# Smaller first input blocks, norm rows and convolution loads moved, and an up weight fetched sooner in a streaming encoder layer

## The chip, the cores and the metric

The kernel runs on one core of a Trainium2 chip. The metric is the time of one execution on the device, in microseconds; several runs are made of a kernel and their median is given. A core has a matrix engine (TensorE, PE in the profile), three engines for elementwise work (VectorE, DVE; ScalarE, ACT; GpSimd, POOL), and SyncE (SP), which here only issues transfers between the device's memory and the on-chip memory. Each engine works through its own list of instructions in order; semaphores make one wait for another. A transfer can be issued from SP's, ACT's or POOL's list.

## The reference

One layer of an encoder is applied to 1024 rows of a prompt and 32 rows of a sample (1056 in all, D = 1024), which share the weights. Cut to what matters:

```python
h = rms_norm(x, g_mix)
q, k, v, ch, cb, cc, ga, gb = split(h @ w_in)
a  = window_attn(q, k, v, sink) @ w_attn_out          # 16 query heads, 4 key heads
bo = (cb * causal_conv3(cc * ch)) @ w_conv_out
x  = x + (sigmoid(ga) * a + sigmoid(gb) * bo) @ w_mix_out
cq = rms_norm(x, g_cross) @ w_cq                      # 4 heads, 256 memory tokens
x  = x + softmax_attn(cq, mem_k, mem_v) @ w_co
x  = x + square(relu(rms_norm(x, g_mlp) @ w_up)) @ w_down
y  = rms_norm(x, g_final)
```

The new keys, values, convolution rows and memory keys and values are returned too. Everything is float32.

## The kernel before

The 1056 columns (tokens lie along the free axis, features on the 128 partitions) are cut into three chunks of 384, 384 and 288 columns, `CH[0]` to `CH[2]`. A float32 product is made of three products of the faster type fp32r: each operand is split into a rounded part hi (a cast on ACT) and the rest lo (a subtraction on DVE), and PE adds hi·hi, hi·lo and lo·hi. So each weight block of 128x1024 goes through a load (tile `wr`), a cast (`wh`, L129) and a subtraction (`wl`, L130), and each activation tile likewise (`X`, `Y`, `N`, `M`, `Z`). `gemm` (L191) makes 8 x 3 matmuls for one output block of 128 features and one chunk.

The stages in order: the input norm and K, V, Q (`norm_x`); windowed attention; the attention's output; the gate products (one pair of gate blocks for each f from 0 to 7; from f = 1 on by a scheme with seven products in place of eight, in which sums of weight blocks, `g_sum`, made earlier on POOL and kept in memory, meet sums of activation tiles, kinds `t2`, `n1`, `n3`, `n4`, `b11` and so on); the convolution's output and the mixing product of each chunk (`do_conv_out`, `do_mix`), woven with the memory attention of the chunk before (`do_cq`, `do_co`); then the up and down products of the MLP, in the same seven-product scheme on halves and quarters of the columns.

`item(fn, *keys)` appends a piece of work to a plan, and the list `worder` of weights that the plan needs is worked off ahead of it: `fetch_w` loads the next weight, `issue_w` splits one. Inside the stages a scheduler orders the instructions of each engine; `pin` keeps an instruction at the place where it is written, and `tc.manual_schedule` does that for all of one engine's. `tile(..., tag, bufs)` takes the next of `bufs` buffers, and waits until that buffer's last reader is done; `acc_tile` gives one of three PSUM accumulators, tag `pt` two further PSUM buffers, `tmp` a scratch buffer (`ct`).

The places that the change touches:

- `norm_x`: loads of x and of the parameters `prm` (gains and other columns), the first weight, the tables of functions of ACT, then the splits and the first products.
- `pump(n)` (L797): splits what the last call loaded, and starts n loads more from the list `wanted`; at the gates these are the tiles of `n4` (from `xs_n`) and then of the convolution (from `bc_d`), that the convolution's output reads. Gate pair f = 1 calls it three times, with 4, 4 and 0.
- The norm of a chunk: `chunk_col` sums the squares on PE into `pq` and works out one number for each column; `chunk_row` spreads it over the partitions (ACT L242, DVE L243, PE L244 and L245 into `pr`, ACT L255 into R). `do_cq` (L1111) multiplies its gemm by R afterwards.
- `do_conv_out` (L1047): a gemm, then the gate's multiplication by L1055 on DVE, the addition L1056, and the split into M. It is L1055 that empties the accumulator.
- `normed(c, f)` (L1285): the normed tile for the MLP by L1287 on DVE, its transfer to memory, and for chunk 0 its split by L1298 (ACT) and L1299 (DVE).
- The order of chunk 2's stage is written out by hand: `then(i, ...)` hangs work behind filler i (fillers 0 to 7 are chunk 2's `do_conv_out`).
- `open_second` and `up_start`: the second set of PSUM tiles and the first up weights; `up_issue(0, 4)` splits one of them. L1362 is ACT's reading of an accumulator of the products before.

Of the kernel before, what the change touches and what calls it, by code (L numbers as in the profile page):

```python
# [40 lines left out]
def hybrid_step(ctx: ExitStack, tc: tile.TileContext, io):  # L41
# [102 lines left out]
    fetched = []  # L144
    third = {}

    def fetch_w():
        if third:
            third["n"] += 1
        if third and third["n"] % 3 == 0:  # L150
            raw = third["pool"].tile([P, 4, 256], F32, tag="ws", name=nm("wr3")).rearrange("p q c -> p (q c)")
        else:
            raw = wp.tile([P, 1024], F32, tag="wr", bufs=2, name=nm("wr"))
        src = weight(worder[wpos[0] + len(fetched)])
        load = sp.dma_start(raw.rearrange("p (i c) -> p i c", i=4) if len(src.shape) == 3 else raw, src)
        if third and third["n"] == 3 and third["pool"] is W["pool"]:
            pin(load)
        fetched.append(raw)
# [130 lines left out]
    start_end = []  # L289

    def norm_x():
        pool_e.memset(ones, 1.0)
        act.copy(ones_r, ones.to_broadcast([P, P]))
        warm = misc.tile([P, 1], F32, name="warm")
        act.activation(warm, ones, AF.Sqrt)
        make_identity(nc, ident)
        raws = []

        def load_x():
            for c, (o, n) in enumerate(CH):  # L300
                raw = raw_tile()[:, : NF * n].rearrange("p (f t) -> p f t", f=NF)
                for h in range(4):
                    sp.dma_start(raw[:, 2 * h : 2 * h + 2], io[f"x{c}"][:, 2 * h : 2 * h + 2])
                    if c == h == 0:
                        sp.dma_start(prm, io["params"])
                if c == 0:
                    fetch_w()
                    fetch_w()
                raws.append(raw)

        def parts(c, fs, pinned=lambda x: x):
            for f in fs:
                xg[c][f] = (slot(xpool, f"X{c}", CH[c][1]), slot(xpool, f"X{c}", CH[c][1]))
                scaled_split(*xg[c][f], raws[c][:, f], G_MIX + f, pinned)

        def squares(c):
            n = CH[c][1]
            acc = st.tile([P, n], F32, tag="sum", bufs=2, name=nm("sum"))
            for f in range(NF):
# [6 lines left out]
        first_raw = wp.tile([P, 1024], F32, tag="wr", bufs=2, name=nm("wr"))  # L326
        with tc.manual_schedule(engines={mybir.EngineType.Activation}):
            act.dma_start(first_raw, weight(worder[0]))
# [24 lines left out]
        for c, (o, n) in enumerate(CH):  # L353
            a = acc_tile([P, n])
            gemm(a, wk, xg[c])
            act.copy(kt[:, o : o + n], a)
            if c < 2:
                parts(c + 1, range(NF), pin)
            vs3[c, 0] = v_block(wv, c, 0)
            if c:  # L360
                scaled(c - 1)
            chunk_col(c)
            vs3[c, 1] = v_block(wv, c, 1)
            vs3[c, 2] = v_block(wv, c, 2)
            if c < 2:
                squares(c + 1)
            if c == 1:
                mem_load_x()
        for key in start_keys:
            next_w(key)  # L370

        def end():
            scaled(2)
            sp.dma_start(io["o_k"][0], kt[:, 896:])
            v = tmp(256)
            sp.dma_start(v, io["cache_v"])
# [537 lines left out]
    def gate_pair(f):  # L914
# [50 lines left out]
        u2 = Y["top"].tile([P, 384], F32, tag="u2", name=nm("u2"))  # L965
        dve.tensor_sub(u2, B, s1)
        sum_step()
        pump(4 if f == 1 else 1)
        w3 = take(("g_sum", f - 1, 1))
        product(C, w3, 1, op("n1"), True)  # L970
        v = Y["top"].tile([P, 384], F32, tag="v", name=nm("v"))
# [75 lines left out]
    def do_conv_out(c, f):  # L1047
        def fn(w):
            n = CH[c][1]
            t1 = tmp(n)  # L1050
            sp.dma_start(t1, m1_d[c][:, f])
            a = acc_tile([P, n])
            gemm(a, w, bcp[c])
            t = tmp(n)
            dve.tensor_mul(t, a, sg[c][f])  # L1055
            (dve if f == NF - 1 else pool_e).tensor_tensor(t, t, t1, op=ALU.add)  # L1056
            mg[c][f] = (mslot(n), mslot(n))
            split(*mg[c][f], t)

        return fn  # L1060
# [50 lines left out]
    def do_cq(c, j):  # L1111
        def fn(w):
            n = CH[c][1]
            a = acc_tile([P, n])
            gemm(a, w, xc[c])
            t = tmp(n)
            dve.scalar_tensor_tensor(t, a, 0.125, R[c], op0=ALU.mult, op1=ALU.mult)
            for e in range(2):
                own, other = slice(64 * e, 64 * e + 64), slice(64 - 64 * e, 128 - 64 * e)
                q = yslot(c)  # L1120
                act.copy(q[own], t[own])
                dve.tensor_sub(q[other], t[own], q[own].bitcast(F32))
                qc[2 * j + e, c] = q

        return fn
# [133 lines left out]
    def open_second():  # L1259
        nonlocal ps  # L1260
        closed(Y["cm", 0])
        closed(ps_cm)
        S["b"] = ctx.enter_context(tc.tile_pool(name="b22", bufs=8, reuse_waits="tile", side="right"))
        L["cm2"], L["pool2"] = opened("late2", bufs=1, reuse_waits="tile", side="right")
        ps = ctx.enter_context(tc.tile_pool(name="ps2", bufs=1, space=PSUM, reuse_waits="tile"))

    def zslot(dt=F32R):
        return S["z"].tile([P, HT], dt, tag="Z", name=nm("Z"))
# [16 lines left out]
    def normed(c, f):  # L1285
        t = tmp(CH[c][1])
        pin(dve.scalar_tensor_tensor(t, x1[c][f], col(G_MLP + f), R[c], op0=ALU.mult, op1=ALU.mult))  # L1287
        o, n = CH[c]
        if c < 2 or f > 3:
            sp.dma_start(xn_d[:, f, o : o + n], t)  # L1290
        if c == 1:
            pool_e.dma_start(xa[1][f][1].bitcast(F32)[:, CH[0][1] - QT :], t[:, : HT - CH[1][0]])
        if c == 2:
            top[f] = t
        if c == 0:
            hi, lo = (yslot(0)[:, :QT] for _ in range(2))
            xa[0][f] = (hi, lo)
            act.copy(hi, t[:, :QT])  # L1298
            pin(dve.tensor_sub(lo, t[:, :QT], hi.bitcast(F32)))  # L1299

    def split_here(hi, lo):

# [318 lines left out]
    def cross_steps(c):  # L1621

        steps = [("call", [])]
        steps.append(("call", [lambda: chunk_stats(c)]))
# [60 lines left out]
    call = lambda fn, *args: lambda: item(lambda: fn(*args))  # L1685
    assert len(left) == 1
    then(0, *[call(x) for x in left[0][1]])
    then(1, call(chunk_stats, 1))
    then(2, *[lambda j=j: item(do_cq(1, j), ("w_cq", j)) for j in range(2)])
    for f in range(NF):  # L1690
        then(f // 2, call(normed, 0, f))
    for i, (_, calls) in zip((3, 5, 7, 9, 11, 12), cross_units(1)):
        then(i, *[call(x) for x in calls])
    then(14, lambda: item(do_co(1, 0), ("w_co", 0)))
# [6 lines left out]
        then(19 + f // 4, call(normed, 1, f))  # L1701
        then(22, call(second_split, f))
    then(19, call(chunk_col, 2))
    then(20, call(chunk_row, 2))
    then(21, lambda: item(do_cq(2, 0), ("w_cq", 0)))
    then(22, lambda: item(do_cq(2, 1), ("w_cq", 1)))
    for i, (_, calls) in zip((23, 25, 26, 28, 29, 31, 32), cross_units(2)):
        then(i, *[call(x) for x in calls])
    then(33, call(open_sums))
# [9 lines left out]
        then(43 + k, call(sums_then, k))  # L1719
    then(41, call(up_ready, 0))  # L1720
    then(43, call(up_second, 0))
    assert len(fillers) == 48
    for i, filler in enumerate(fillers):
        item(*filler)
# [4 lines left out]
    def up_start():  # L1729
        open_second()  # L1730
        up_load(0)
        up_issue(0, 4)
        second_b22()
        up_issue(0, 3)
        up_ready(1)
        up_second(1)
        up_t2(0)
# [258 lines left out]
```

## Time and profile before

| | |
|---|---|
| median of 3 runs | 1757.81 us (1757.32 to 1761.07) |
| the profiled execution | 1754.54 us |
| its span in the profile | 1752.8 us |
| granted TensorE clock, mean | 0.997 |
| PE busy | 1724.4 us, 98% |
| DVE busy | 1190.7 us, 68% |
| ACT busy | 853.7 us, 49% |
| POOL busy | 583.9 us, 33% |

A row of the waits gives the engine, what it was about to do, what released it, and then the total in us, the number of waits and the longest. A row of the time line gives start, duration (both in us), engine, line, operation, output<-inputs, sizes and a count where equal rows are taken together; in brackets stands the idle time of that engine before the instruction and what ended it. PEld is the load of a weight into PE, ACTq and SPq are issues of transfers. Matmuls overlap, so the time that one takes of PE is the distance of two starts, not its duration. A row of the windows gives the stretch and its length, the busy time of PE, PEld, DVE, ACT and POOL with their instructions, then PEclk (the granted clock, 1.00 is full), the DMA engines' share and GB/s.

### The profile page before, as it was taken

Reading aid. Unit: us, or ns where it says so; the run is one execution under the profiler, and the core shown is the slowest. Engines: PE = TensorE matmul, PEld = TensorE weight load, DVE = VectorE, ACT = ScalarE, POOL = GpSimd, SP = SyncE. Lnnn points to the kernel's source line nnn. Section 1 sums busy time; section 2 is a strip of 40 time slices with the busy share of each in tenths; the row PEclk is TensorE's granted clock in tenths of the full one; section 3 lists DMA queues with packets and bytes.
Section 4 is the critical chain, followed back from the end, with each engine's and each line's share of the span. In section 5 each row is a group of like instructions: output and inputs, shape, how many; then the busy total and the mean of one; then the engine's idle time right before and its main releaser. Section 6 shows DMA issues by size and latency. Waiting matters only on the chain.

```text
span 1752.8 us, 32573 instructions
## 1 busy us (share of the span) xinstructions
PE 1724.4 (98%) x12250; PEld 1710.3 (98%) x12250; DVE 1190.7 (68%) x2275; ACT 853.7 (49%) x1661; POOL 583.9 (33%) x667
## 2 busy tenths in 40 slices
PE   8999999999999999999999999999999999999998
PEld 8999999999999999999999999999999999999998
DVE  6776776867666656545677878787666686545675
ACT  8653533535335324334556665765444463332443
POOL 0025366443543444441225132105555410000121
PEclk9999999999999999999999999999999999999999
DMA  5243344333436888857866667775666695555554
GB/s 185 93 124 126 126 133 139 127 131 132 159 135 197 291 301 294 285 195 232 279 211 199 222 219 233 236 261 179 220 223 219 220 328 186 189 191 173 188 170 159
DMA packets 179565, 346.60 MB, mean 198 GB/s; under 512 B 18624, under 2 KB 100832, under 8 KB 179280
## 3 DMA queue, kind: packets, MB, share of 16 engines
q1 hardware_dynamic: 163360, 289.73, 50.1%
q0 software_dynamic: 15568, 53.68, 8.7%
q8 instruction: 96, 1.57, 0.4%
q10 hardware_dynamic: 480, 1.11, 0.2%
q14 instruction: 61, 0.50, 0.1%
HBM read 250.73 MB, written 93.14 MB: 196 GB/s over the span
## 4 chain that ended last, share of the span: by engine, by line
PE 53%; DMA 3%; DVE 2%; ACT 1%; POOL 1%; issue 1%; SPq 0%; DVEq 0%; POOLq 0%; ACTq 0%
PE acc L1781 6%; PE acc L1782 6%; PE acc L1783 6%; PE acc L870 6%; PE acc L871 6%; PE acc L872 6%; PE acc L196 2%; PE acc L198 2%; PE acc L197 2%; PE pc L871 2%; PE pc L872 2%; PE pc L870 2%; DMA ct<-in_x 1%; DMA ct<-m_d 1%; POOL ct L1056 1%
## 5 line engine op out<-in xcount | busy, mean ns | idle before, releaser
L129 ACT CAST wh<-wr 128x1024 fp32r<-128x1024 f32 (+1 forms) x231 | 241.6, 1046 | 411.8 <-PE acc L1782 132.2
L130 DVE TENSOR_TENSOR wl<-wr,wh 128x1024 fp32r<-128x1024 f32 (+1 forms) x231 | 295.6, 1280 | 129.5 <-ACT wh L129 127.7
L196 PE MATMUL acc<-X,wh 128*128 128x384 f32 (+1 forms) x864 | 282.7, 327 | 7.0 <-ACT wh L129 7.0
L197 PE MATMUL acc<-X,wh 128*128 128x384 f32 (+1 forms) x864 | 279.9, 324 | 0.3 <-DVE X L276 0.3
L198 PE MATMUL acc<-X,wl 128*128 128x384 f32 (+1 forms) x864 | 278.8, 323 | 0.0
L272 POOL TENSOR_TENSOR xacc<-xacc,ct 128x384 f32<-128x384 f32 (+1 forms) x56 | 76.9, 1376 | 374.9 <-ACT ct L270 373.3
L196 PEld LDWEIGHTS acc<-X,wh 128*128 128x128 f32 x864 | 163.3, 189 | 7.9 <-ACT wh L129 7.0
L197 PEld LDWEIGHTS acc<-X,wh 128*128 128x128 f32 x864 | 163.6, 189 | 1.4 <-DVE X L276 0.7
L198 PEld LDWEIGHTS acc<-X,wl 128*128 128x128 f32 x864 | 163.4, 189 | 0.1
L196 PE MATMUL acc<-Y,wh 128*128 128x384 f32 (+1 forms) x432 | 139.2, 324 | 3.4 <-DVE ct L1055 3.4
L197 PE MATMUL acc<-Y,wh 128*128 128x384 f32 (+1 forms) x432 | 139.2, 323 | 0.4 <-DVE Y L781 0.3
L198 PE MATMUL acc<-Y,wl 128*128 128x384 f32 (+1 forms) x432 | 139.2, 323 | 0.0
L1782 PE MATMUL acc<-n,wh 128*128 128x264 f32 x352 | 100.2, 285 | 0.0
L129 ACT CAST PTh<-pt 128x512 fp32r<-128x512 f32 (+3 forms) x94 | 45.9, 516 | 111.4 <-PE pt L588 110.6
L1781 PE MATMUL acc<-n,wh 128*128 128x264 f32 x352 | 100.2, 285 | 0.0
L1783 PE MATMUL acc<-n,wl 128*128 128x264 f32 x352 | 99.9, 284 | 0.0
L725 POOL TENSOR_TENSOR xacc<-xacc 128x256 f32<-128x256 f32 x100 | 87.9, 879 | 5.6 <-DMA xacc<-in_w_in 0.3
L725 POOL TENSOR_TENSOR ws<-ws 128x256 f32<-128x256 f32 x100 | 87.1, 871 | 5.6
L196 PEld LDWEIGHTS acc<-Y,wh 128*128 128x128 f32 x432 | 81.0, 188 | 4.5 <-DVE ct L1055 4.2
L197 PEld LDWEIGHTS acc<-Y,wh 128*128 128x128 f32 x432 | 81.1, 188 | 1.0 <-DVE Y L781 1.0
L198 PEld LDWEIGHTS acc<-Y,wl 128*128 128x128 f32 x432 | 81.1, 188 | 0.3 <-DMA wl<-wl_d 0.3
L574 ACT ACTIVATE S<-S,nmx 128x257 f32<-128x257 f32 (+1 forms) x132 | 64.2, 488 | 19.8 <-DVE nmx L569 18.5
(426 smaller groups left out, 5511.0 us busy)
## 6 DMA issues: line engine op xcount, KB each, us to landing
wr<-in_w_up SPq DMA_DIRECT2D x53, 512.0 KB, 4.7
wr<-in_w_in SPq DMA_DIRECT2D x52, 512.0 KB, 3.8
wr<-wsum_d SPq DMA_DIRECT2D x40, 512.0 KB, 3.5
wr<-in_w_conv_out SPq DMA_DIRECT2D x24, 512.0 KB, 4.1
wr<-in_w_mix SPq DMA_DIRECT2D x24, 512.0 KB, 4.9
wr<-in_w_down SPq DMA_DIRECT2D x24, 512.0 KB, 3.5
n_d<-Z SPq DMA_DIRECT2D x32, 264.0 KB, 4.3
xacc<-in_w_down POOLq DMA_DIRECT2D x16, 512.0 KB, 4.4
```

Of the source, the lines that this page charges most:

```text
L129: act.copy(hi, src)
L130: dve.tensor_sub(lo, src, hi.bitcast(F32))
L196: pe.matmul(out, wh[:, a], hi, start=(k == 0), stop=False)
L197: pe.matmul(out, wh[:, a], lo, start=False, stop=False)
L198: pe.matmul(out, wl[:, a], hi, start=False, stop=(k == len(acts) - 1))
L725: pin(pool_e.tensor_tensor(t[:, to], t[:, x], t[:, y], op=ALU.add))
L870: pe.matmul(acc, wh[:, a], hi, start=(start and k == 0), stop=False, skip_group_check=True)
L871: pe.matmul(acc, wh[:, a], lo, start=False, stop=False, skip_group_check=True)
L872: pe.matmul(acc, wl[:, a], hi, start=False, stop=(k == 3), skip_group_check=True)
L1781: pe.matmul(a, wh[:, s], hi, start=(t == 0 and k == 0), stop=False, skip_group_check=True)
L1782: pe.matmul(a, wh[:, s], lo, start=False, stop=False, skip_group_check=True)
L1783: pe.matmul(a, wl[:, s], hi, start=False, stop=(t == 1 and k == 7), skip_group_check=True)
```

## The change

Five edits, at separate places:

1. At the start, x's first block comes in transfers of one, one, two, two and two of its eight tiles; `prm` and the first weight (in two pieces) are issued from ACT's list ahead of the loading of its tables; four matmuls of plain float32 on a constant tile (`spin`) stand first on PE; the third weight goes to a `ws` tile.
2. In the gate pair f = 1 the second call of `pump` goes, so that the `bc_d` tiles start with f = 2.
3. `chunk_row` of a chunk is called inside `do_cq`, behind its first gemm, and no longer ahead of it.
4. For chunk 2, L1055 is pinned; the eight `normed` of chunk 0 hang behind fillers 1 to 8, one each, where two hung behind each of fillers 0 to 3; their lo part moves from DVE to POOL.
5. `up_issue(0, 4)` moves from `up_start` to filler 44, and two PSUM tiles that nothing uses are taken at the end of `open_second`.

```diff
+    def fetch_w(raw=None):          # with raw given, the weight is loaded there
...
     def norm_x():
+        spin = tmp(384)
+        dve.memset(spin, 1.0)
+        for _ in range(4):
+            pe.matmul(acc_tile([P, 384]), spin[:, :P], spin, start=True, stop=True)
         pool_e.memset(ones, 1.0)
-        act.copy(ones_r, ones.to_broadcast([P, P]))
+        first_raw = wp.tile([P, 1024], F32, tag="wr", bufs=2, name=nm("wr"))
         warm = misc.tile([P, 1], F32, name="warm")
-        act.activation(warm, ones, AF.Sqrt)
+        with tc.manual_schedule(engines={mybir.EngineType.Activation}):
+            act.dma_start(prm, io["params"])
+            for at in (slice(0, 256), slice(256, 1024)):
+                act.dma_start(first_raw[:, at], weight(worder[0])[:, at])
+            act.copy(ones_r, ones.to_broadcast([P, P]))
+            act.activation(warm, ones, AF.Sqrt)
...
-                for h in range(4):
-                    sp.dma_start(raw[:, 2 * h : 2 * h + 2], io[f"x{c}"][:, 2 * h : 2 * h + 2])
-                    if c == h == 0:
-                        sp.dma_start(prm, io["params"])
+                for a in (0, 1, 2, 4, 6) if c == 0 else (0, 2, 4, 6):
+                    b = a + 1 if c == 0 and a < 2 else a + 2
+                    sp.dma_start(raw[:, a:b], io[f"x{c}"][:, a:b])
                 if c == 0:
                     fetch_w()
-                    fetch_w()
+                    fetch_w(W["pool"].tile([P, 4, 256], F32, tag="ws", ...)...)
...
-        with tc.manual_schedule(engines={mybir.EngineType.Activation}):
-            act.dma_start(first_raw, weight(worder[0]))
...
         sum_step()
-        pump(4 if f == 1 else 1)
+        if f > 1:
+            pump(1)
         w3 = take(("g_sum", f - 1, 1))
...
-            dve.tensor_mul(t, a, sg[c][f])
+            (pin if c == 2 else lambda x: x)(dve.tensor_mul(t, a, sg[c][f]))
...
             gemm(a, w, xc[c])
+            if j == 0:
+                chunk_row(c)
...
         ps = ctx.enter_context(tc.tile_pool(name="ps2", ...))
+        ps.tile([P, 512], F32, tag="pt", bufs=2, name=nm("pc"))
+        wide_tile()
...
-            pin(dve.tensor_sub(lo, t[:, :QT], hi.bitcast(F32)))
+            pool_e.tensor_tensor(lo, t[:, :QT], hi.bitcast(F32), op=ALU.subtract)
...
-    then(1, call(chunk_stats, 1))
+    then(1, call(chunk_col, 1))
...
-        then(f // 2, call(normed, 0, f))
+        then(1 + f, call(normed, 0, f))
...
-    then(20, call(chunk_row, 2))
-    then(21, lambda: item(do_cq(2, 0), ("w_cq", 0)))
-    then(22, lambda: item(do_cq(2, 1), ("w_cq", 1)))
+    then(20, lambda: item(do_cq(2, 0), ("w_cq", 0)))
+    then(21, lambda: item(do_cq(2, 1), ("w_cq", 1)))
...
+    then(44, call(up_issue, 0, 4))
...
     def up_start():
         open_second()
         up_load(0)
-        up_issue(0, 4)
```

How instructions stand on three lists shows what moved. First SP's in the gate pair f = 1, before:

```order
238 L805 DMA ct_8065<-bc_d_89 128x384
239 L155 DMA wr_8160<-gsum_d 128x1024
240 L926 DMA m_d_92<-ct_7953 128x384
241 L805 DMA ct_8067<-bc_d_89 128x384
242 L805 DMA Gb_1350_7993<-xs_n_112 128x384
243 L926 DMA m_d_94<-ct_8022 128x288
244 L805 DMA Gb_1351_7995<-xs_n_112 128x384
245 L805 DMA ct_8069<-bc_d_89 128x384
246 L805 DMA ct_8071<-bc_d_89 128x384
```

and now:

```order
238 L935 DMA m_d_92<-ct_7965 128x384
239 L814 DMA Gb_1355_8005<-xs_n_112 128x384
240 L935 DMA m_d_94<-ct_8034 128x288
241 L814 DMA Gb_1356_8007<-xs_n_112 128x384
242 L943 DMA ct_8178<-a_d_107 128x384
243 L159 DMA wr_8201<-in_w_in 128x1024
```

The four loads of `bc_d` around the two loads of `xs_n` (L805 before, L814 now) are gone from here. Second PE's, the first `do_cq` gemm of chunk 0 (`pr` is the spread norm row), before:

```order
5400 L196 MATMUL acc_1823_10314<-Y0_1769_10099,wh_1794_10200 128x384
5401 L244 MATMUL pr_1808_10254<-ct_1809_10255,ones_r_75 128x384
5402 L197 MATMUL acc_1823_10314<-Y0_1770_10100,wh_1794_10200 128x384
5403 L198 MATMUL acc_1823_10314<-Y0_1769_10099,wl_1795_10201 128x384
5404 L245 MATMUL pr_1808_10254<-ct_1810_10256,ones_r_75 128x384
```

and now:

```order
5415 L200 MATMUL acc_1835_10365<-Y0_1726_9915,wh_1813_10267 128x384
5416 L248 MATMUL pr_1826_10339<-ct_1827_10340,ones_r_75 128x384
5417 L201 MATMUL acc_1835_10365<-Y0_1727_9916,wh_1813_10267 128x384
5418 L202 MATMUL acc_1835_10365<-Y0_1726_9915,wl_1814_10268 128x384
5419 L200 MATMUL acc_1835_10365<-Y0_1739_9966,wh_1813_10267 128x384
```

The product that makes `pr` stood in the first gemm and stands now in the next one (another accumulator), 15 rows later. Third DVE's, around one of chunk 2's multiplications (L1055 before, L1065 now), before:

```order
1166 L1299 TENSOR_TENSOR Y_2037_11240<-ct_11236,Y_2036_11239 128x264
1167 L1287 SCALAR_TENSOR_TENSOR ct_11243<-Ga_1708_9852,prm,R_11223 128x384
1168 L1055 TENSOR_TENSOR ct_11283<-acc_11258,Ga_1390_8187 128x288
1169 L234 SCALAR_TENSOR_TENSOR rc_11290<-st_t_11298,st_y_11297 128x3
1170 L130 TENSOR_TENSOR wl_11414<-wr_11411,wh_11413 128x1024
1171 L1299 TENSOR_TENSOR Y_2040_11247<-ct_11243,Y_2039_11246 128x264
```

and now:

```order
1169 L238 SCALAR_TENSOR_TENSOR rc_11288<-st_t_11296,st_y_11295 128x3
1170 L1301 SCALAR_TENSOR_TENSOR ct_11303<-Ga_1701_9815,prm,R_11235 128x384
1171 L1065 TENSOR_TENSOR ct_11343<-acc_11318,Ga_1415_8351 128x288
1172 L247 SCALAR_TENSOR_TENSOR ct_11384<-ident,rc_11288,ct_11383 128x128 x3
1173 L130 TENSOR_TENSOR wl_11405<-wr_11402,wh_11404 128x1024
1174 L130 TENSOR_TENSOR M_11347<-ct_11343,M_11346 128x288
```

The split of `normed` (L1299) has left DVE's list, and one product of `normed` (L1287 before, L1301 now) stands ahead of the multiplication.

More of the change, by code (lines that the diff above doesn't have):

```diff
@@ L145, in hybrid_step @@
     third = {}
-    def fetch_w():
-        if third:
+    def fetch_w(raw=None):
+        if raw is not None:
+            pass
+        elif third:
             third["n"] += 1
-        if third and third["n"] % 3 == 0:
+        if raw is not None:
+            pass
+        elif third and third["n"] % 3 == 0:
             raw = third["pool"].tile([P, 4, 256], F32, tag="ws", name=nm("wr3")).rearrange("p q c -> p (q c)")
@@ L301, in load_x @@
                 raw = raw_tile()[:, : NF * n].rearrange("p (f t) -> p f t", f=NF)
-                for h in range(4):
-                    sp.dma_start(raw[:, 2 * h : 2 * h + 2], io[f"x{c}"][:, 2 * h : 2 * h + 2])
-                    if c == h == 0:
-                        sp.dma_start(prm, io["params"])
+                for a in (0, 1, 2, 4, 6) if c == 0 else (0, 2, 4, 6):
+                    b = a + 1 if c == 0 and a < 2 else a + 2
+                    sp.dma_start(raw[:, a:b], io[f"x{c}"][:, a:b])
                 if c == 0:
                     fetch_w()
-                    fetch_w()
+                    fetch_w(W["pool"].tile([P, 4, 256], F32, tag="ws", name=nm("ws")).rearrange("p q c -> p (q c)"))
                 raws.append(raw)
@@ L324, in squares @@
             accs[c] = [acc]
-        first_raw = wp.tile([P, 1024], F32, tag="wr", bufs=2, name=nm("wr"))
-        with tc.manual_schedule(engines={mybir.EngineType.Activation}):
-            act.dma_start(first_raw, weight(worder[0]))
         fetched.append(first_raw)
@@ L1623, in cross_steps @@
         steps = [("call", [])]
-        steps.append(("call", [lambda: chunk_stats(c)]))
+        steps.append(("call", [lambda: chunk_col(c)]))
         steps.append(("items", [(do_cq(c, j), ("w_cq", j)) for j in range(2)]))
```

## The prediction

> **What bounds the kernel now.** I read the page's busy times first, then the waits of PE, then the time line at each wait, and the windows last.
>
> ```profile
> span 1752.8 us, 32573 instructions
> ...
> PE 1724.4 (98%) x12250; PEld 1710.3 (98%) x12250; DVE 1190.7 (68%) x2275; ACT 853.7 (49%) x1661; POOL 583.9 (33%) x667
> ```
>
> PE is busy for 1724.4 of 1752.8 us. The change leaves the reference's matmuls as they are and adds four, so it can only act on the 28 us in which PE is not busy, and on stretches at a lower clock. The waits of PE name where those 28 us lie:
>
> ```profile
> PE acc L196 <- ACT wh L129: 7.0, 1, 7.0
> PE acc L196 <- DVE ct L1055: 3.4, 3, 1.9
> PE acc L870 <- ACT lt L1362: 2.2, 1, 2.2
> PE pr L244 <- ACT ct L242: 1.7, 1, 1.7
> PE acc L870 <- DVE Ga L988: 1.5, 1, 1.5
> PE acc L870 <- ACT wh L129: 1.2, 1, 1.2
> ```
>
> These six rows hold 17 us in eight places, and every edit of the diff stands at one of them. A wait is seldom the whole loss: the first matmul behind it also runs longer. The profiled execution took 1754.54 us, 1.7 more than its span, and 3.3 less than the median of the runs shown (1757.81). I make the sum as a difference and take it off the median. From 0.2% on (3.5 us) a difference can be told from none.
>
> **Part 1, the start.**
>
> ```profile
> 0.73 0.41 ACTq L328 DMA_DIRECT2D wr<-in_w_in  x1
> ...
> 4.06 0.20 ACT L295 ACTIVATE warm<-ones 128x1 f32<-128x1 f32 x1
> ```
> ```profile
> 6.08 0.61 ACT L275 ACTIVATE X<-raw,prm 128x384 fp32r<-128x384 f32 x1 [1.82 <-DMA prm<-in_params]
> 6.61 1.12 ACT L129 CAST wh<-wr 128x256 fp32r<-128x256 f32 x2
> ```
> ```profile
> 6.73 0.62 DVE L276 SCALAR_TENSOR_TENSOR X<-raw,prm,X 128x384 fp32r<-128x384 f32 x1 [0.54 <-ACT X L275]
> 7.27 1.45 DVE L130 TENSOR_TENSOR wl<-wr,wh 128x256 fp32r<-128x256 f32 x2
> 8.64 3.79 DVE L276 SCALAR_TENSOR_TENSOR X<-raw,prm,X 128x384 fp32r<-128x384 f32 x7
> ```
> ```profile
> 7.05 0.69 PE L196 MATMUL acc<-X,wh 128*128 128x384 f32 x1 [7.05 <-ACT wh L129]
> ...
> 10.11 0.52 PE L196 MATMUL acc<-X,wh 128*128 128x384 f32 x1
> 10.43 0.52 PE L197 MATMUL acc<-X,wh 128*128 128x384 f32 x1
> ...
> 15.10 0.33 PE L198 MATMUL acc<-X,wl 128*128 128x384 f32 x1
> 15.27 0.28 PE L206 MATMUL acc<-wh,X 128*128 128x256 f32 x1
> ```
> ```profile
> 1050.56 0.81 PE L227 MATMUL pq<-ones,ct 128*128 128x1 f32 x6
> ```
>
> ACT waited 1.82 us for `prm`, which stood behind 384 KB of `raw` on SP's queue. Then X (0.53 us to the start of wh) and wh had to be made before PE could start at 7.05. Now `prm` goes first, and before the first product lie 192 KB of x and 128 KB of weight in place of 384 and 512. So the transfers should land near 4 us, and ACT itself becomes the limit: its work on the function tables ended at 4.26 (4.06 + 0.20), and two more DMA issues ahead of that, at 0.41 us each, make it 5.1. From there the same 0.97 us (6.08 to 7.05) leads to a first product at about 6.05: 1.0 us gained.
>
> The larger part is the clock. In the first gemm the matmuls start 0.32 us apart (10.11, 10.43), at its end 0.17 (15.10, 15.27): the 24 products took from 7.05 to 15.27, most of it at half pace. The four added matmuls fill PE from about 1.2 us on. They are plain fp32, and the trace has none of 384 columns: from 0.32 us each (the fp32r row) to 1.28 (four such passes), four take 1.3 to 5.1 us. I take the upper end: plain fp32 products leave two records each (the last row is three `pq` products), and I allow each record the columns twice. If PE is then at full speed when X arrives, the gemm is bound by DVE's lo parts instead: the first X lo can start at 5.75 (6.73 less the gain), and 0.62, 1.45 for the two pieces of wl and 3.79 for the other seven X make 11.6; PE's three products of the last X are over at 12.1, against 15.27. Next comes w_v, late by some 0.4 because its wl stands on DVE behind them. So 3.2 less 0.4 gives 2.8 us. After that PE runs gapless (29.00 busy of 29.00, the first row), so the gain is carried whole. Bounds: 1.0 if the fillers warm nothing; a loss of 0.5 if they end behind the first X.
>
> ```profile
> 15.00:44.00 29.00, 29.00 (x230) 29.00 (x229) 21.94 (x55) 24.48 (x64) 1.02 (x1) 1.00 0.34 128
> 1052.20:1055.60 3.40, 3.40 (x16) 3.40 (x15) 0.84 (x5) 1.13 (x2) 0.33 (x1) 0.50 0.42 145
> 1140.90:1144.30 3.40, 3.40 (x18) 3.40 (x17) 2.86 (x10) 1.91 (x3) 0.00 (x0) 0.51 1.02 411
> ```
>
> [...]
>
> **Part 2, the first gate pair (f = 1).**
>
> ```profile
> 677.47 0.51 ACT L800 CAST N<-Gb 128x384 fp32r<-128x384 f32 x1 [5.53 <-DMA Gb<-xs_n]
> 677.89 1.04 ACT L129 CAST wh<-wr 128x1024 fp32r<-128x1024 f32 x1
> ```
> ```profile
> 683.96 2.56 DVE L801 TENSOR_TENSOR Y<-ct,Y 128x384 fp32r<-128x384 f32 x2
> 686.43 0.54 DVE L988 TENSOR_TENSOR Ga<-acc,s 128x384 f32<-128x384 f32 x1
> ```
>
> ACT stood 5.53 us at a cast of N whose load SP had issued behind the loads of `bc_d`; the cast of wh queued behind it and PE stood 1.2 us (the last of the six rows). Seven us later DVE split two of those same `bc_d` tiles in 2.56 us, with L988 behind them, and PE stood 1.5 (the row above it). Without `bc_d` in this pair both causes go: 1.2 + 1.5, and with the longer first matmuls behind them about 0.6 more, 3.3. The eight loads and splits move to later pairs, two for each, in which none of the six rows above has a wait. Next late is N itself if its load still takes its 6 us, so I take 2.8, between 1.2 (the second wait stays) and 3.3.
>
> **Part 3, the norm row behind the first query product.**
>
> ```profile
> 889.83 0.45 PE L244 MATMUL pr<-ct,ones_r 128*128 128x384 f32 x1 [1.72 <-ACT ct L242]
> ```
>
> PE stood 1.72 us at `pr`, with gemm products that needed nothing of it behind. `pr` now comes 15 rows later in the same stream; at 0.17 us each (15.10 to 15.27 above) that is 2.6 us, which covers the wait. What reads R, the multiplication of `do_cq`, comes behind the gemm anyway. I take 1.7; bounds 0 (the row is late for R, and PSUM comes free late) and 2.0.
>
> **Part 4, the convolution's output of chunk 2** (L1055 pinned, one `normed` for each item, the lo part of it on POOL).
>
> ```profile
> 1000.50 0.82 DVE L1055 TENSOR_TENSOR ct<-acc,Gb 128x288 f32<-128x288 f32 x2
> ...
> 1001.01 0.40 PE L196 MATMUL acc<-Y,wh 128*128 128x288 f32 x1 [1.86 <-DVE ct L1055]
> 1001.09 0.81 POOL L1056 TENSOR_TENSOR ct<-ct,ct 128x288 f32<-128x288 f32 x1 [6.89 <-DVE ct L1055]
> ```
>
> L1055 frees the accumulator of a gemm, and PE waited for it three times, 3.4 us (1.86 the longest), with restarts about 3.9. Ahead of it on DVE stood the split and the product of `normed`. The split goes to POOL, eight of them; the trace has none there. The nearest row is L1056's own, 0.81 us for 288 columns, and so eight of 264 cost at most 6.5 us of POOL; DVE wins the time of its eight. Who waits for POOL: L1056 queues behind a split, and behind that the split of M and the mixing gemm, several items later. With one `normed` ahead of L1055 in place of two, I expect one of the three waits to be left in part: 2.4 gained, bounds 3.9 and -2 (rival 2).
>
> **Part 5, the up weight.**
>
> ```profile
> 1176.11 0.39 ACT L1362 ACTIVATE lt<-acc 128x264 f32<-128x264 f32 x1
> ```
>
> The first up product needed the PSUM bank that L1362 was the last to read, and L1362 stood behind two casts of a weight on ACT. The two placeholders turn the banks, so that it takes the bank which the read before that leaves, and its own weight is cast earlier. The 2.2 us go; next are the casts of the second weight, which are no earlier than before. I take 2.0, bounds 0 and 2.4.
>
> **The clock later on** I leave out of the sum. At two places PE falls to half clock for 3.4 us, each worth 1.7 us (the rows from 1052.2 and from 1140.9 above, PEclk 0.50 and 0.51). PE was not waiting there or just before; small products of one column came ahead of both. Nothing in the change takes these away, but everything shifts by some us, so one may come or go: 1.7 either way.
>
> **The sum:** 2.8 + 2.8 + 1.7 + 2.4 + 2.0 = 11.7 us. 1757.8 - 11.7 = 1746.1, rounded to 1746.
>
> **The rivals.**
>
> 1. *The middle gives back* (0.2). Between 960 and 1200 us the norms, `normed` and the memory attention of three chunks are mixed anew on all engines, and a wait may merely move. Then parts 4 and 5 bring nothing and 2.8 + 2.8 + 1.7 = 7.3 is left: 1750.5. For it: DVE is busy at 68% over all and the gaps there are single L1055s behind other work. Against it: the bank of part 5 doesn't depend on DVE.
>
> 2. *POOL becomes the late one, slower* (0.15). Eight splits of `normed` stand on POOL, in order, each behind its ACT cast. If each holds L1056 by its own 0.8 us plus the wait for that cast, the mixing gemms of chunk 2 meet late M tiles: eight waits of 1.86 us, the longest of now, are 14.9. With the 7.3 of parts 1 to 3 and nothing from parts 4 and 5 that is 7.6 slower, 1765.4. It decides from 0.9 us for each split on (eight of 0.9 use up the 7.3). Against it: POOL waited 6.89 us before its L1056, so it has room there now.
>
> 3. *The fillers don't do what they are for* (0.1): PE is still slow when X comes. Part 1 is then 1.0, the sum 9.9: 1747.9. With a loss of 0.5 there, 1749.4.
>
> **How the numbers follow.** My forecast, 0.55, has its own range of 1741 (all upper bounds, 3.2 + 3.3 + 2.0 + 3.9 + 2.4 = 14.8, and one half-clock stretch less) to 1752 (part 2 at 1.2, part 4 at none, one stretch more: 2.8 + 1.2 + 1.7 + 2.0 - 1.7 = 6.0). Nine tenths of it lie in there, 0.50, and rivals 1 and 3 almost whole, 0.27; to come to 0.8 the range goes on to 1757, a third of the way to rival 2: 1741 to 1757. Faster by over 0.2% is below 1754.3: all of the forecast, nine tenths of rivals 1 and 3, less 0.04 for parts of the forecast that fail together: 0.78. Slower is rival 2 at a little less than its whole, 0.14. The rest, 0.08, is no change.
>
> **What would show it.** In the profile of the changed kernel: first real product at 6.0 to 6.3 and the first gemm's matmuls 0.17 apart; no wait of L870 on L988 or wh near 676 to 685; no wait of `pr` near 885; at most one wait on L1055 over 1 us; no wait of 2 us at the first up product. A first gemm still 0.32 apart, or POOL rows of the new split as releasers of PE's waits for M, would make it wrong.

## The result, and the profile after

The changed kernel takes 1761.67 us in the median of 22 runs (1755.51 to 1766.14), the kernel before 1757.07 in 22 runs beside them. The ratio is 1.0023 with a 95% interval of 1.0014 to 1.0033: it is 4.1 us slower (2.5 to 5.8), where I had forecast 11.7 us faster. The two profiled executions lie 8.7 us apart, so a stage's loss in them is larger than in the mean. Ratios of the runs below are turned into us with 1756 us.

The page of the changed kernel first, and then PE's waits:

```profile
span 1761.5 us, 32594 instructions
...
PE 1734.7 (98%) x12258; PEld 1714.5 (97%) x12258; DVE 1193.1 (68%) x2268; ACT 852.0 (48%) x1661; POOL 602.4 (34%) x675
```
```profile
PE acc L202 <- DMA wl<-wl_d: 2.9, 1, 2.9
PE acc L200 <- ACT X L279: 2.0, 1, 2.0
PE acc L200 <- ACT M L129: 1.8, 1, 1.8
PE acc L879 <- DVE Ga L1080: 1.4, 1, 1.4
PE acc L299 <- DVE ct L297: 1.3, 1, 1.3
PE acc L879 <- ACT wh L129: 1.0, 1, 1.0
```

Of the six waits that the prediction began with, those for the first wh (7.0), for `pr` (1.7), for L988 (1.5) and for L1362 (2.2) are gone, the three on L1055 are one of 0.4, and a wait for a wh of 1.0 stands 8 us later than the one of 1.2. In their place stand waits for the second X, for M, for `Ga`, and for a weight's lo part. How much later the matmul at the same place of PE's list begins after than before (the four fillers left out of the count):

| place (before, us) | later by, us | what lies ahead of it |
|---|---|---|
| 18 to 120 | +1.0 to +1.2 | the start |
| 588 | +0.9 | no edit of the change |
| 690 to 837 | -0.6 | gate pair f = 1 |
| 891 | +2.7 | a wait of 2.9 for `wl`, and half clock behind it |
| 989 | +0.7 | the waits on L1055 that went |
| 1030 | +7.5 | the convolution and the mixing product of chunk 2 |
| 1190 | +7.2 | the wait for L1362 that went, and two of 0.4 and 0.8 that came |
| 1227 to the end | +9.2 to +9.0 | three waits between 1203 and 1207 (their time after) |

**The start.** PE's time line, then one row of ACT's, then the windows of 8.0 to 11.5 us:

```profile
1.32 4.82 PE L299 MATMUL acc<-ct 128*128 128x384 f32 x8 [1.32 <-DVE ct L297]
6.09 0.44 PE L200 MATMUL acc<-X,wh 128*128 128x384 f32 x1
6.46 0.44 PE L201 MATMUL acc<-X,wh 128*128 128x384 f32 x1
6.79 0.44 PE L202 MATMUL acc<-X,wl 128*128 128x384 f32 x1
9.23 0.69 PE L200 MATMUL acc<-X,wh 128*128 128x384 f32 x1 [2.00 <-ACT X L279]
...
16.24 0.28 PE L210 MATMUL acc<-wh,X 128*128 128x256 f32 x1
```
```profile
7.83 0.83 ACT L129 CAST wh<-wr 128x768 fp32r<-128x768 f32 x1 [1.78 <-DMA wr<-in_w_in]
```
```profile
8.00:8.70 0.70, 0.00 (x0) 0.00 (x0) 0.01 (x1) 0.70 (x2) 0.00 (x0) 1.00 1.06 432
8.70:9.20 0.50, 0.00 (x0) 0.00 (x0) 0.50 (x1) 0.50 (x2) 0.00 (x0) 0.53 1.00 412
9.00:11.50 2.50, 1.96 (x5) 1.56 (x6) 2.50 (x5) 2.50 (x6) 0.00 (x0) 0.50 1.02 415
```

The first product starts at 6.09 (forecast 6.05), and the fillers end in time. But ACT's order is fixed here, and next in it stands the cast of the other 768 columns of the first weight. That piece landed only at 7.7 us, ACT stood 1.78 us for it, and the second X stood behind it. PE idled 2.0 us, its clock fell to half at 8.7, and the gemm went on at 0.32 us a matmul until 15.5.

**Chunk 2's convolution.** The window of 1005 to 1037 us, where most is lost:

```profile
1005.00:1037.00 32.00, 26.58 (x180) 23.44 (x179) 26.75 (x50) 19.77 (x46) 10.47 (x11) 1.00 0.54 172
```

PE is busy for 26.58 of 32 us here; before, it was 32.00 in the same stretch. The last product of `normed` for chunk 0 stood on DVE at 1000 before; the time line of DVE now has it 24 us later:

```profile
999.98 0.61 DVE L1287 SCALAR_TENSOR_TENSOR ct<-Gb,prm,R 128x384 f32<-128x384 f32 x1
```
```profile
1024.24 0.61 DVE L1301 SCALAR_TENSOR_TENSOR ct<-Gb,prm,R 128x384 f32<-128x384 f32 x1
```

### The profile page after: what moved, and what is told of

It reads as the page before. It is cut to its first block, busy times and chain, and to the rows that moved or that the text cites. A ratio compares the mean times of both kernels' runs of the same rounds, so it can differ in the third digit from the quotient of the medians.

```text
span 1761.5 us, 32594 instructions
## 1 busy us (share of the span) xinstructions
PE 1734.7 (98%) x12258; PEld 1714.5 (97%) x12258; DVE 1193.1 (68%) x2268; ACT 852.0 (48%) x1661; POOL 602.4 (34%) x675
## 4 chain that ended last, share of the span: by engine, by line
PE 52%; DMA 4%; DVE 2%; ACT 1%; issue 1%; POOL 1%; SPq 0%; DVEq 0%; POOLq 0%; ACTq 0%
PE acc L1794 6%; PE acc L1795 6%; PE acc L1796 6%; PE acc L879 6%; PE acc L881 6%; PE acc L880 6%; PE acc L200 2%; PE acc L202 2%; PE acc L201 2%; PE pc L879 2%; PE pc L881 2%; PE pc L880 2%; DMA ct<-in_x 2%; DMA ct<-m_d 1%; DVE wl L130 1%
## 5 line engine op out<-in xcount | busy, mean ns | idle before, releaser
L734 POOL TENSOR_TENSOR ws<-ws 128x256 f32<-128x256 f32 x100 | 94.8, 948 | 5.7
```

The costliest lines, as they stand in the source:

```text
L734: pin(pool_e.tensor_tensor(t[:, to], t[:, x], t[:, y], op=ALU.add))
```

## The experiments

All runs are timed beside the kernel before. An interval of some 2 us to either side is left on each, so that only differences beyond that are told from none.

**Each part alone, on the kernel before.** The edits are those of the diff in the section on the change, one part at a time.

```diff
# e1_start: part 1, all edits of norm_x and fetch_w, of them
+            for at in (slice(0, 256), slice(256, 1024)):
+                act.dma_start(first_raw[:, at], weight(worder[0])[:, at])
# e2_gate: part 2
-        pump(4 if f == 1 else 1)
+        if f > 1:
+            pump(1)
# e3_row: part 3, with chunk_col for chunk_stats, of it
+            if j == 0:
+                chunk_row(c)
# e4_conv: part 4
+            (pin if c == 2 else lambda x: x)(dve.tensor_mul(t, a, sg[c][f]))
+            pool_e.tensor_tensor(lo, t[:, :QT], hi.bitcast(F32), op=ALU.subtract)
+        then(1 + f, call(normed, 0, f))
# e5_up: part 5, of it
+    then(44, call(up_issue, 0, 4))
```

> Only part 1 (the start) on top of the kernel before. Theory A (each part does alone what the two traces show at its place): the first gemm is over about 1.0 us later than before, since ACT casts 768 columns of the weight's second piece, which lands at 7.7 us, ahead of all further X, PE idles 2.0 us after three products and its clock falls back: +1 us in all. Rival B (what was lost arose from the five parts together): the first gemm is over 2.8 us earlier, as forecast: -2.8 us.

> Only part 2 (no second pump at f = 1). Theory A: the waits near 679 and 687 shrink by 1.5 to 2 us in all, and the gain is given back at about 872, where PE comes to a part of a weight (wl from memory) that lands at its own time: between -0.5 and +2 us over the whole. Rival B: -2.8 us, still there at 1000 us.

> Only part 3 (the norm row behind the first query product). Theory A: the wait of 1.7 us for pr at 890 goes and nothing comes in its place before 1000; between 1000 and 1100 chunk 2's cq stands one filler earlier, and what that does there is open: -2 to +1 us. Rival B: -1.7 us, no new wait over 1 us.

> Only part 4 (L1055 pinned for chunk 2, one normed for each filler, its lo part on POOL). Theory A: the three waits on L1055 shrink by 3 to 4 us, but M of chunk 2 comes late at the first mixing product and several waits of 0.5 to 3 us follow to 1037: +3 to +5 us in all. Rival B: -2.4 us.

> Only part 5 (two unused PSUM tiles taken, the first up weight's split at filler 44). Theory A (as the trace of the changed kernel shows at its place): the wait of 2.2 us for L1362 at 1176 goes, and four waits of 0.5 to 1 us come between 1184 and 1207: +0.5 to +2 us. Rival B (the wait at 1176 is not in every execution, since two runs with that place unchanged lack it): the gain is smaller than the 2.0 forecast, and the time is within 1 us of before.

| run | median, us | ratio (95%) | us |
|---|---|---|---|
| e1_start | 1757.7 | 1.0003 (0.9991 to 1.0014) | +0.5 (-1.6 to +2.5) |
| e2_gate | 1752.42 | 0.998 (0.9967 to 0.9993) | -3.5 (-5.8 to -1.2) |
| e3_row | 1755.03 | 0.9989 (0.9975 to 1.0003) | -1.9 (-4.4 to +0.5) |
| e4_conv | 1762.25 | 1.003 (1.0015 to 1.0045) | +5.3 (+2.6 to +7.9) |
| e5_up | 1755.1 | 0.9993 (0.9982 to 1.0005) | -1.2 (-3.2 to +0.9) |

Part 4 loses by itself, and part 2 gains by itself. In the trace of e2_gate, against that of the kernel before, PE is 0.1 us late ahead of the gate pair, 2.0 us ahead behind it, still 2.0 ahead at 960, and 2.6 near the end. The wait of theory A does come (1.3 us for `wl` at 871), but the wait for `pr` behind it is shorter by as much; the time of the whole is theory B's. The five add up to -0.8, against +4.1 measured; with five errors of 2 to 3 us each that gap alone proves nothing.

**What in part 4 costs.** It has three edits: the pin of L1055, the spread of `normed` over fillers 1 to 8, and the lo part on POOL.

```diff
# e6_pinspread
+            (pin if c == 2 else lambda x: x)(dve.tensor_mul(t, a, sg[c][f]))
+        then(1 + f, call(normed, 0, f))
# e7_pool: of part 4, the line of pool_e alone
# e7_pinpool: the lines of pin and of pool_e
```

> Part 4 without the POOL split: L1055 pinned and one normed of chunk 0 for each of the fillers 1 to 8. Theory A (the loss of 5.3 us of part 4 lies in the spread: DVE meets normed, the memory attention and M in the same fillers, and SP's loads of m_d stand behind the stores of normed): +4 to +6 us. Rival C (it lies in POOL, where L1056 stands behind the splits): 0 to -2 us.

> Part 4's POOL split alone: L1299 on POOL, L1055 not pinned, normed two by two as before. Theory A (the spread costs): -1 to +1 us, with the waits on L1055 smaller than before. Rival C (POOL costs): +3 to +5 us, with waits of PE for M behind L1056.

> Part 4 without the spread: L1055 pinned and L1299 on POOL, normed two by two as before. Theory A: -1 to -3 us, with at most one wait on L1055 over 1 us. Rival C: +3 to +5 us.

e6_pinspread took 1.0035 (1.0023 to 1.0047), +6.1 us; e7_pool 0.9998 (0.9987 to 1.0009) and e7_pinpool 0.9998 (0.9989 to 1.0007), both -0.4. So the spread is the loss, and POOL is not. Nor did the pin gain: in e7_pinpool's trace one wait on L1055 of 0.8 us is left, and one of 1.7 for M stands where none was.

**By what the spread costs.** Either by the order of SP's list, or by DVE's work:

```diff
# s1_store, on e6_pinspread
-            sp.dma_start(xn_d[:, f, o : o + n], t)
+            (pool_e if c == 0 else sp).dma_start(xn_d[:, f, o : o + n], t)
# s2_offdve, on e4_conv; a1_offdve, on the changed kernel
+        if c == 0:
+            pool_e.tensor_tensor(t, x1[c][f], R[c], op=ALU.mult)
+            act.mul(t, t, col(G_MLP + f))
+        else:
             pin(dve.scalar_tensor_tensor(t, x1[c][f], col(G_MLP + f), R[c], ...))
```

> The spread with its pin (+5.5 us alone), the lo part on DVE, and the stores of the spread normed tiles issued from POOL's list in place of SP's. Theory F (SP's loads of m_d and of weights stand behind stores that wait for normed): the loss goes, -1 to +1 us. Theory G (DVE has too much to do in the later fillers, beside the memory attention): still +4 to +6 us.

> The spread as in part 4, but the product of normed for chunk 0 is made by POOL (times R) and ACT (times the gain) in place of DVE; its lo part is on POOL. Theory F: still +4 to +6 us. Theory G: the loss goes for the larger part, -1 to +2 us.

> The changed kernel with one edit: for chunk 0 the product of normed is made by POOL (times R) and ACT (times the gain) in place of DVE; the spread stays. Theory G (it is DVE's load in the later fillers that the spread cost): the waits of 0.4 to 3 us between 1005 and 1037 shrink by half or more, and the time is -2 to -5 us against the kernel before, where the changed kernel is +4. Rival F (the order of SP's list): +2 to +4 us.

s1_store: 1.0017 (1.0007 to 1.0027), +3.0 us, between the two theories. s2_offdve: 0.9978 (0.9967 to 0.9989), -3.9 us, where e4_conv is +5.3. a1_offdve: 0.9999 (0.999 to 1.0009), -0.2 us, where the changed kernel is +4.1. The window of 1005 to 1037 of s2_offdve, and then of a1_offdve:

```profile
1005.00:1037.00 32.00, 30.95 (x225) 30.11 (x224) 28.82 (x50) 23.23 (x49) 15.92 (x14) 1.00 0.70 233
```
```profile
1005.00:1037.00 32.00, 31.82 (x234) 31.22 (x234) 29.66 (x52) 24.89 (x52) 15.65 (x15) 1.00 0.71 239
```

With eight products of 0.61 us taken off DVE, four of which stood in this window, PE got back 5.2 of the 5.4 us that it lacked here; some of it a1_offdve pays earlier, where PE is busy for 18.60 of the 20 us from 985 on, against 20.00 in the changed kernel.

The whole stretch shows the cause better, with one trace of each kernel. From 960 to 1045 us PE falls behind the kernel before by 4.9 to 8.4 us in the five kernels that have the spread with its products on DVE (the changed kernel, e4_conv, e6_pinspread, s1_store, u2_nostart), by 0.4 to 0.8 in the three that have the spread with the products on POOL and ACT (a1_offdve, s2_offdve, b3_best), and by -1.3 to +2.5 in the eleven others. Theory G holds for the place. Whether it is the products' time or their places in DVE's list that PE pays for, these runs do not separate. As a whole s2_offdve came out better than theory G said and a1_offdve worse; the latter has another cause, below.

SP's order shows no share at the place: s1_store loses 7.0 us there and e6_pinspread 8.4, and e6_pinspread's trace has a stretch at half clock there (1005.6 to 1009.0, worth 1.7) that s1_store's lacks. In the whole time their intervals overlap, and a small share of it stays open.

**Taking back parts of the changed kernel.** u1_nospread has `normed` where it was, u2_nostart the old start.

```diff
# u1_nospread
-        then(1 + f, call(normed, 0, f))
+        then(f // 2, call(normed, 0, f))
# u2_nostart: part 1 taken back
```

> The changed kernel with normed of chunk 0 two by two behind the fillers 0 to 3 as before; all else changed. Theory A (the spread is the loss and the parts add up; alone they gave 0.5 for the start, -3.5 for the gate, -1.9 for the row, -0.8 for pin and POOL, -1.2 for the up weight): -4 to -7 us against the kernel before. Rival D (the parts take each other's gain, as the whole change is some 5 us slower than the sum of its parts): -1 to +1 us.

> The changed kernel with the start as before. Theory A: the start alone cost 0.5, so +3 to +4 us against the kernel before. Rival D (the start's shift spoils what comes behind): -1 to +1 us.

u1_nospread: 0.9983 (0.9971 to 0.9994), -3.0 us. u2_nostart: 0.9995 (0.9984 to 1.0005), -0.9. So the spread cost the changed kernel 7.1 us and the start 5.0, more than alone (6.1 and 0.5), each with an error of 2 to 3 us. u1_nospread lies between theory A and D, and u2_nostart where theory D put it.

**The start.**

```diff
# m2_nospin, on e1_start
-        for _ in range(4):
-            pe.matmul(acc_tile([P, 384]), spin[:, :P], spin, start=True, stop=True)
# m1_start, on e1_start
-            for at in (slice(0, 256), slice(256, 1024)):      # on ACT's list
+            act.dma_start(first_raw[:, :256], weight(worder[0])[:, :256])
...
+                    if c == 0 and a == 1:
+                        sp.dma_start(first_raw[:, 256:], weight(worder[0])[:, 256:])
...
+            # the second X is made between the two pieces of the first weight
```

> The kernel before with a mended start: as part 1, but the second piece of the first weight (768 columns) is loaded from SP's list behind the first two blocks of x, and ACT makes the second X before it casts that piece. Theory A (the start lost because ACT stood at that cast until the piece landed, so that PE idled and its clock fell): PE stays at full clock, the first gemm is over near 12.5 us, -2 to -3 us. Rival E (the lo parts on DVE and the landing of x bind it anyway, and the clock falls back): 0 to -1 us.

> Part 1 without the four fillers. Theory A (the warmth of the fillers is lost while PE idles before the second X): the first gemm ends where it does with them, within 0.7 us, and the time is that of part 1 alone within 1 us. Rival E (they are worth something already): 1.5 to 2 us slower than part 1 alone.

The first V product, which ends the first gemm, starts in twelve traces with the old start at 14.03 to 15.27 us (mean 14.4), in four with the new one at 15.60 to 16.93 (mean 16.4), without the fillers at 16.33, and in three with the mended one at 12.17 to 12.82 (mean 12.4). So part 1 costs 1.9 us at its place, the fillers are worth nothing there (theory A, from one trace without them), and the mended start gains 2.0. PE's time line of m1_start, and its window to be set against the changed kernel's:

```profile
8.96 0.45 PE L200 MATMUL acc<-X,wh 128*128 128x384 f32 x1 [1.51 <-ACT X L279]
...
12.82 0.28 PE L210 MATMUL acc<-wh,X 128*128 128x256 f32 x1
```
```profile
9.00:11.50 2.50, 2.17 (x11) 1.77 (x12) 2.50 (x6) 2.44 (x5) 0.00 (x0) 1.00 1.02 415
```

PE still waits, 1.51 us, but its clock stays full, and eleven matmuls begin where five did. Yet as a whole m1_start is at 1.0008 (0.9993 to 1.0022), +1.4 us, and m2_nospin at 1.002 (1.0008 to 1.0031), +3.5, which is 3.0 us slower than e1_start, where theory A allowed 1 (the two intervals overlap). What m1_start gained at 13 us was not there at the end.

**All that gained, together.** b1_all: the mended start, parts 2, 3 and 5, pin and POOL without the spread. b2_oldstart: the same with the old start. b3_best: the changed kernel with the mended start and with `normed` off DVE.

```diff
# b1_all = m1_start + e2_gate + e3_row + e7_pinpool + e5_up
# b2_oldstart = e2_gate + e3_row + e7_pinpool + e5_up
# b3_best = a1_offdve + the mended start
```

> All that looked good: the mended start, no second pump at f = 1, the norm row behind the first query product, pin and POOL split without the spread, the up weight. Theory A (gains add up): -3.0 (the changed kernel without the spread) and 2 to 3 less for the start: -5 to -7 us. Rival H (what PE gains early, it waits away at the next load that lands at its own time): -2 to -4 us.

> The same with the start as before. Theory A: the first V product stands some 1.5 us earlier than with the changed start, so -4 to -6 us. Rival H: -2 to -4 us, like the changed kernel without the spread.

> The same with the mended start. Theory G with kept gains: -5 to -8 us against the kernel before. Rival H (early gains are waited away at loads that land at their own time): -2 to -5 us, like the one without the mended start.

b1_all: 1752.18 us, 0.9978 (0.9966 to 0.999), -3.9. b2_oldstart: 0.9997 (0.9986 to 1.0009), -0.5. b3_best: 1751.09 us, 0.9982 (0.997 to 0.9994), -3.2. The gains don't add: each of the first and third has four gains in it, and they are no faster than the gate alone or s2_offdve alone. These two lie in rival H's range, b2_oldstart is slower than either theory said. The wait that rival H names, for `wl` near 870, is 1.1 us in b1_all, 1.6 in b2_oldstart and 0.5 in b3_best, and the trace of before has none. Another reason shows in the traces. The waits of PE in e7_pool between 1180 and 1205 us are these; in e7_pinpool the same stretch has none:

```profile
PE pc L871 <- DVE b L1305: 1.0, 2, 0.7
PE acc L870 <- DVE Z L1510: 0.8, 1, 0.8
PE pc L870 <- DVE Z L1531: 0.6, 1, 0.6
```

Neither kernel edits anything there. But the scheduler has put the up products into another order, on PE and on DVE. DVE's list there in e7_pinpool and then in e7_pool:

```
1498 L1495 TENSOR_TENSOR Z_14571<-acc_2722_14546,lt_14508 128x528
1499 L1531 TENSOR_TENSOR Z_14395<-pc_14473,Z_14395 128x264
1500 L1531 TENSOR_TENSOR Z_14395<-pc_14474,Z_14395 128x264
1501 L130 TENSOR_TENSOR wl_14676<-wr_2708_14402,wh_14675 128x1024
1502 L1559 TENSOR_TENSOR lt_14324<-acc_2703_14370,lt_14324 128x528
1503 L1536 TENSOR_TENSOR Z_14616<-Z_14395,Z_14536 128x528
1504 L130 TENSOR_TENSOR wl_14719<-s_2729_14582,wh_14718 128x1024
```
```
1499 L1495 TENSOR_TENSOR Z_14571<-acc_2722_14546,lt_14508 128x528
1500 L1531 TENSOR_TENSOR Z_14395<-pc_14473,Z_14395 128x264
1501 L1531 TENSOR_TENSOR Z_14395<-pc_14474,Z_14395 128x264
1502 L1559 TENSOR_TENSOR lt_14324<-acc_2703_14370,lt_14324 128x528
1503 L130 TENSOR_TENSOR wl_14676<-wr_2708_14402,wh_14675 128x1024
1504 L130 TENSOR_TENSOR wl_14719<-s_2729_14582,wh_14718 128x1024
1505 L1536 TENSOR_TENSOR Z_14616<-Z_14395,Z_14536 128x528
```

In seven of the twenty kernels DVE's last 560 rows stand in this second order, the changed kernel among them, with m1_start, e7_pool, a1_offdve, b1_all, b2_oldstart and b3_best; all seven have these waits. The stretch of PE's list that takes 32.0 us before (from 1183 to 1215) takes 35.1 in each of the seven, so the order goes with 3.1 us. Twelve have the first order, none of them has the waits, and the stretch takes 32.0 to 32.4. (u2_nostart has a third order and 33.2.) That is a match over twenty traces, not a trial of that order by itself, which wasn't made. It is about as large as the gate's gain, and the mended start, b1_all and b3_best carry it to the end.

## Why the prediction was wrong

**Part 1: the step that failed is the sum of DVE's lo parts.** The prediction's terms 0.62, 1.45 and 3.79 took every X as there in time. It had quoted ACT's cast of wh as one row of two casts, and didn't ask when the second piece lands: 7.7 us, with SP's loads of x under way beside it (418 GB/s from 7 to 9 us). It measured +1.9 us at the place for a forecast of -2.8. The first product itself and the fillers' end came as worked out. The prediction used the clock for the warming and not for the fall: in the changed kernel the clock fell to half in a wait of 2.0 us, and was at half from 8.7 to 15.5 us. That the fillers bring PE to full speed was its assumption, which no run had shown by then; in the changed kernel the clock was full from 5.31 us on. The upper end of 5.1 us for the four fillers was an estimate too; they took 4.8, with their records 0.64 us apart at half clock, twice the 0.32 of an fp32r row.

**Part 2: right in its direction, its next wait wrong.** Both named waits are gone in all eight traces with part 2. What came next was not N but another cast of wh, 1.0 us in each of them (the row in the list above is one). The first of the named waits was also that one execution's: five of the eleven other traces without part 2 have no wait for a wh there, though nothing at that place is edited. From 665 to 692 us the eight are 1.2 us shorter in the mean than the twelve without part 2, for a forecast of 2.8. -3.5 alone (-5.8 to -1.2).

**Part 3: right in its cause.** The wait of 1.7 for `pr` is gone after. The 15 rows of the prediction are a difference of two list numbers, and the fillers at the head of the list shift these; within the gemms `pr` moved by 12 products, 2.1 us at 0.17, which still covers the wait. But in the twelve traces without part 3 that wait is 0 to 2.3 us, 0.9 in the mean, so 1.7 was high. -1.9 alone, of which the interval leaves open that it is nothing.

**Part 4: wrong in sign.** -2.4 was forecast, +5.3 measured. The step that failed is "one `normed` ahead of L1055 in place of two": the waits on L1055 did shrink, from 3.4 to 0.4, but the work did not go, it went to fillers 4 to 8, where DVE also has the memory attention, M and the splits of weights, and PE waits there in turn (1004 to 1040 us: 1.8 for M, 1.4 for `Ga`, 0.5 for `uh`, 0.4 for L1065, and three of 0.3). Rival 2 had the sign and the place, and the wrong engine: it had POOL, which alone measured -0.4 us (e7_pool), and DVE was the one (s2_offdve, a1_offdve); that it had the sign was luck. The trace of before held a warning: DVE was busy for 28.76 of the 32 us from 1005 on, a row that the prediction does not have. That leaves 3.2 us, and four of the products, 2.4 us, came to stand there:

```profile
1005.00:1037.00 32.00, 32.00 (x240) 31.84 (x239) 28.76 (x55) 23.16 (x49) 10.86 (x11) 1.00 0.67 226
```

**Part 5: not settled.** The 2.2 us for L1362 are gone after at that product; 0.4 for the same line (L1376 there) stand 2 us behind it. But e2_gate and e3_row, without part 5, lack that wait as well, and b2_oldstart, with it, has 1.5 us of it. In the twelve traces without part 5 that wait is 0 to 2.2 us, 1.1 in the mean: a wait that comes and goes from kernel to kernel was priced as if it were fixed. -1.2 alone (-3.2 to +0.9).

**The clock** was left out with 1.7 to either side. In the changed kernel's profile a stretch at half clock came at 876, behind the wait of 2.9 us for `wl`:

```profile
874.78 0.44 PE L202 MATMUL acc<-Y,wl 128*128 128x384 f32 x1 [2.91 <-DMA wl<-wl_d]
...
876.11 0.52 PE L202 MATMUL acc<-Y,wl 128*128 128x384 f32 x1
```

That wait is 0.8 to 1.9 us in kernels that are edited only behind that place (e4_conv to e7_pinpool, s1_store, s2_offdve), and none in the trace of before, m1_start and u1_nospread, so it goes with no single part. With its half clock it is some 4.6 us of the 8.7 by which the profiled pair is apart; how much of that is in the mean, one trace of each does not tell.

**The sum.** Adding five gains assumed that each stays to the end. The traces show the order of the up products changed by edits that have nothing to do with it, at 3.1 us: m1_start edits only the start, over 1100 us ahead of it. And the prices of parts 2, 3 and 5 were waits of one execution, that other kernels with the same code at the place have smaller or not at all.

## What to carry to other kernels

Where work is moved to be out of the way of one wait, read how busy its engine is at the place it goes to, in a window over that place; here its row left little more room than the moved work needed (3.2 us for 2.4). Where an engine's order is written out by hand at a start, each item waits for its own data, as ACT here stood 1.78 us for the second piece: write down when each piece lands, not only the first. And where a scheduler orders the rest, compare its order over the whole program, since an edit can cost more far behind than it gains in its place (m1_start gained 2.0 us at 13 us, and its stretch from 1183 on took 3.1 more). And where a wait is to be priced, look at it in more than one trace.

## What the runs showed of the hardware that was not expected

PE's clock fell to half behind waits of 2.0, 2.2, 2.3 and 2.8 us at 9 us (the changed kernel, a1_offdve, u1_nospread, e1_start) and of 2.9 us at 872 (the changed kernel), and stayed full behind waits of 1.5, 0.75 and 0.72 us at 9 us (m1_start, b1_all, b3_best). The length of a wait alone does not decide: before, it stayed full behind one of 2.2 us that ended at 1176.6, and fell at 1052.19 and 1140.94 us, with no wait of PE there or just ahead (busy for 3.00 of 3.00 us from 1049 on and for 3.70 of 3.70 from 1137 on). The first changes of the clock in the changed kernel's trace are at 5.31, 8.73, 15.55 and 875.71 us, so 3.41, 6.83 and 860.16 us apart; in the trace of before they are at 14.54, 1052.19, 1055.60, 1140.94 and 1144.35 us, so 1037.65, 3.41, 85.33 and 3.41 apart. Each of these distances is within 0.01 us a whole multiple of 3.4133 (1, 2 and 252 times; 304, 1, 25 and 1). So the place of a wait against these steps may count beside its length; no run tried that by itself.

Four plain fp32 matmuls of 384 columns took from 1.32 to 6.1 us, in eight records, in the changed kernel's trace; from the second on they begin 0.64 us apart at half clock, and the last two 0.33 apart at full clock. In the seven traces with them PE's clock was full from 5.3 to 6.8 us on, in the twelve with the old start from 11.8 to 14.5 (before, 14.54), and with the new start without them from 14.4: with them it was full 5 us sooner, or more.
